# MLP gate and up projections: from feature-major blocks to token-major groups of 512 + 512 columns

## The chip, the cores and the metric

The kernel runs on one core of one Trainium2 chip. The metric is the device time of one execution in microseconds (us). The five engines have queues of their own and run side by side: TensorE (PE) multiplies, VectorE (DVE) and ScalarE (ACT) work element by element, GpSimd (POOL) does a few small things, SyncE (SP) starts most transfers. The kernel is written on a layer that puts in the semaphores and sets the order of the instructions on each engine, with the order of the program as priority.

## The reference, cut to what matters

One encoder layer on 256 tokens, D_MODEL = 2048, D_FF = 5632, all float32:

```python
proj = rms_norm(x, attn_norm) @ w_in                  # 2048 -> 10240, then two attentions ya, yb
merged = sigmoid(ga) * (ya @ w_branch_a) + sigmoid(gb) * (yb @ w_branch_b)
x = x + merged @ w_out
hf = rms_norm(x, ffn_norm)
g = dwconv_centred(hf @ w_ffn_gate, conv_w, conv_b)   # width 3 along the tokens
x = x + (gelu(g) * (hf @ w_ffn_up)) @ w_ffn_down
x = x + sigmoid(rms_norm(x, ple_norm) @ w_ple_gate) * (p @ w_ple_proj)
out = rms_norm(x, final_norm)
```

## The kernel before, in words

**Products from halves.** A float32 operand is split into a high half in the matmul's reduced format and a low half, the difference. A product is then high x high + high x low + low x high. Weights arrive in pieces of 1 MB ([128 x 2048] float32, a ring of three, `raw`), loaded by SP. `produce` (L244) makes each piece's units: ScalarE copies a stretch into a high half (L261), VectorE subtracts it from the weights for the low half (L262). Units stand in a ring of six (`u`), and, for weight differences, a ring of two (`v`). A unit is dropped when its last product is issued, and `pump` (L267) then makes the next ones.

**Two forms of product.** In `block` (L284) the weights are the stationary operand, [128 x 128], and the activations move: 512 columns (high and low half of 256 tokens side by side) for the high weights, 256 for the low ones. The result is feature-major: features in the partitions, tokens along the row. In `thirds` (L321) the activations stand, 128 tokens at a time, and 512 columns of weights move, three matmuls of 512 columns. The result is token-major.

**Seven for eight.** `quad_stage` (L331) works on two output ranges of 512 columns and 256 tokens at once. A piece covers two blocks of 128 rows (k) for both ranges. A plain piece ("s") has 8 products of `thirds`; a piece by seven products ("S") has 7 into seven banks (M1 to M7), but needs differences of the weights (units T13 and T24 from L254 to L256, ring `v`) and sums of the activations (`sums_of`, L780, called `combine` or made on the way). `row_sums` (L750) adds the banks at the stage's last piece and hands each [128 x 512] result to a `finish` function, two or more products after it is done. `at(stage, piece, product)` puts such work at a place in PE's order, `run_due` runs it.

**Stages.** A: the input projection and attention. B0 to B3: the gates in `quad_stage`, B0 all plain, B1 to B3 with the pattern "SsSsSsSs", each followed by the branch products. D0, D1: the output projection, the same pattern; the sums go into `xr`, the residual in token-major rows. Four `turn_back` calls (L803; four transposes of 128 x 128 into bank P22, then copies that split) turn a half of the rows into the feature-major `hf`. E0: half of the MLP's 44 feature chunks; F00, F01: its down projection (11 pieces, "SsSsSsSsSss"); E1, F10, F11 the other half. Then the per-layer embedding (pp, G) and the last norm.

**E before.** `_ffn` (L97) lists gate and up chunks in turn; each is 16 calls of `block` into a bank, 704 a half. `mlp` (L916) gathers the two halves of a bank (ScalarE and VectorE), multiplies by the norm's factor spread over all partitions, does the convolution along the row with per-partition taps, the gelu, the product and the split into `act`, 256 columns at a time. The first four chunks of E0 go side by side, while the second half of `hf` is turned.

Of the kernel before, what the change touches and what calls it, by code (L numbers as in the profile page):

```python
# [32 lines left out]
FHALF = FC // 2  # L33
# [54 lines left out]
JOINT = 4  # L88
# [4 lines left out]
DOWN = "SsSsSsSsSss"  # L93
STANDARD = "s" * 8


def _ffn(half):  # L97

    jobs = []
    for f in range(FHALF + 1):  # L100
        if f < FHALF:
            jobs.append(("g", half * FHALF + f))
        if f:
            jobs.append(("u", half * FHALF + f - 1))
    return jobs


def _pieces():
# [23 lines left out]
    for j in range(4):  # L132
        quads("B%d" % j, ("w_in", GA * P + j * WIDE), ("w_in", GB * P + j * WIDE), ALT if j else STANDARD)
        wide("ba%d" % j, ("w_branch_a", j * WIDE), QH)
        wide("bb%d" % j, ("w_branch_b", j * WIDE), HG)
    for s in range(2):
        quads("D%d" % s, ("w_out", 2 * s * WIDE), ("w_out", (2 * s + 1) * WIDE), ALT)
    for half in range(2):
        names = {"g": "w_ffn_gate", "u": "w_ffn_up"}
        jobs = [(names[kind], f) for kind, f in _ffn(half)]  # L140
        joint = 0 if half else JOINT
        e = [(name, k, f) for k in range(KC) for name, f in jobs[:joint]]
        e += [(name, k, f) for name, f in jobs[joint:] for k in range(KC)]
        blocks("E%d" % half, e)
        for s in range(2):
            quads("F%d%d" % (half, s), ("w_ffn_down", 2 * s * WIDE), ("w_ffn_down", (2 * s + 1) * WIDE),
                  DOWN, half * FHALF)
# [14 lines left out]
def _unit_list():  # L162

    units, of = [], []
    for p, (kind, _) in enumerate(_PIECES):
        if p == 0:
            cuts = [("n", a * P, b * P) for a, b in ((0, 3), (3, 7), (7, 11), (11, PIECE))]
        elif kind == "S":
            cuts = [("n", 0, WIDE), ("n", 2 * WIDE, 4 * WIDE), ("T13", 0, 2 * WIDE), ("T24", 2 * WIDE, 4 * WIDE)]
        else:  # L170
            cuts = [("n", 0, 2 * WIDE), ("n", 2 * WIDE, 4 * WIDE)]
        of.append(list(range(len(units), len(units) + len(cuts))))
        units += [(p, *cut) for cut in cuts]
# [8 lines left out]
RINGS = {"u": 6, "v": 2}  # L182


@with_exitstack
def _encoder(ctx: ExitStack, tc, xt, pt, xrow, cols, gainrow, table, onehot, mask, ident_in, wts, out):
# [57 lines left out]
    def produce():  # L244
# [6 lines left out]
        ring = "u" if kind == "n" else "v"  # L251
# [10 lines left out]
        nc.vector.tensor_tensor(lo, src, hi.bitcast(F32), op=ALU.subtract)  # L262
# [4 lines left out]
    def pump():  # L267
        while not state["early"] and state["unit"] < len(_UNITS):
            p, kind = _UNITS[state["unit"]][:2]
            if state["u" if kind == "n" else "v"] <= 0 or kind != "n" and "tok" not in held:  # L270
                break
# [7 lines left out]
    def drop(u):  # L279
        del made[u]  # L280
        state["u" if _UNITS[u][1] == "n" else "v"] += 1
# [49 lines left out]
    def quad_stage(stage, moving, combos=None, tags=("M2", "M3", "M4", "P22")):  # L331
# [11 lines left out]
        for p in pieces:  # L343
            kind = _PIECES[p][0]
            for name in (list(tags) * 2 if kind == "s" else ["M1", "M7", "M5", "M6", "M2", "M3", "M4"]):
# [10 lines left out]
        for i, p in enumerate(pieces):  # L356
# [3 lines left out]
            if kind == "s":  # L360
# [41 lines left out]
    def gather(acc, scale=1.0, u=None, keep=lambda ins: ins):  # L402

        t = sc.tile([P, T], F32, name="t")
        keep(nc.scalar.activation(t, acc[:, T:], AF.Copy, scale=scale))
        if u is None:
            u = sc.tile([P, T], F32, name="u")
# [17 lines left out]
    def sums(total, columns):  # L425

        s = bank("misc", P, len(columns))
        for c, tokens in enumerate(columns):
            nc.tensor.matmul(s[:, c:c + 1], total[:, tokens], ones[:, :1], start=True, stop=True)
# [10 lines left out]
    def diagonal(r):  # L440

        dg = sc.tile([P, T], F32, name="rdg", bufs=1)
# [4 lines left out]
    def spread(key, dg):  # L447
# [3 lines left out]
        rt[key] = sc.tile([P, T], F32, name="rms", bufs=1)  # L451
# [298 lines left out]
    def row_sums(stage, last, finish, strassen=True, ready=None):  # L750
# [3 lines left out]
        def first():  # L754
            c = outputs()
            if strassen:
                a = held["accs"]
                nc.scalar.activation(c[0][:, cut[0]], a["M1"], AF.Copy)
                nc.vector.tensor_tensor(c[0][:, cut[1]], a["M6"], c[0][:, cut[0]], op=ALU.add)
                nc.vector.tensor_tensor(c[1][:, cut[0]], a["M7"], c[0][:, cut[1]], op=ALU.add)  # L760
                nc.vector.tensor_tensor(c[0][:, cut[1]], a["M5"], c[0][:, cut[1]], op=ALU.add)
                nc.vector.tensor_tensor(c[1][:, cut[1]], a["M5"], c[1][:, cut[0]], op=ALU.add)
# [11 lines left out]
    def quads(stage, moving, combos, finish, strassen=True, ready=None):  # L774
        last = len(_STAGES[stage]) - 1
        row_sums(stage, last, finish, strassen, ready)
# [3 lines left out]
    def sums_of(u, tag):  # L780

        tok = held["tok"]
        f = tok.tile([P, 4, P], F32, name="cmb")
# [12 lines left out]
    def combine(key, m, pair, tag):  # L796

        u = held["tok"].tile([P, 2, T], F32, name="pair", bufs=2)
# [32 lines left out]
    at(("B0", 4, 0), open_tok)  # L831
    for i in range(0, 8, 2):
        at(("B0", 4 + i // 2, 4), combine, "hs", hs, i, i // 2)
    rh = halved(rc[0])

    for j in range(4):

        def gated(t, n, a):
            c = held["c"][t][:, cut[n]]
            if j:  # L840
                nc.vector.tensor_tensor(c, a, c, op=ALU.add)
                a = c
# [7 lines left out]
        quads("B%d" % j, lambda k: hs[:, k, :], lambda i: combos["hs", i], gated, j > 0)  # L850
# [18 lines left out]
    def residual(stage, s, moving, key, square):  # L869
# [14 lines left out]
        quads(stage, moving, lambda i: combos[key, i], finish, True, ready)  # L884
# [18 lines left out]
    for pair, which in enumerate(("M2", "M3", "M4", "P22")):  # L903
        at(("E0", 2 + pair), rows_pair, which, 4 + pair, hf, 1)

    def norm_columns():
        at(("E0", 11), spread, 1, diagonal(rows_root()))

    at(("E0", 8), norm_columns)

    def activation_row(k):
        k %= FHALF
        tile, k = (held["act"][0], k) if k < 16 else (held["act"][1], k - 16) if k < 20 else (held["act"][2], k - 20)
        return tile[:, k, :]

    def mlp(kind, n, acc):  # L916
        tok = held["tok"]
        if kind == "g":
            if n % 2 == 0:
                held["gw"] = tok.tile([P, 4, T], F32, name="gw", tag="c%d" % (n // 2 % 2 + 1))  # L920
            c, w = (held["gw"][:, 2 * (n % 2) + i] for i in range(2))
            u = gather(acc)
            nc.vector.tensor_tensor(u, u, rt[1], op=ALU.mult)
            nc.vector.tensor_scalar(c, u, tap(1, n), tap(3, n), op0=ALU.mult, op1=ALU.add)
            nc.vector.scalar_tensor_tensor(c[:, 1:], u[:, :-1], tap(0, n), c[:, 1:], op0=ALU.mult, op1=ALU.add)
            nc.vector.scalar_tensor_tensor(c[:, :-1], u[:, 1:], tap(2, n), c[:, :-1], op0=ALU.mult, op1=ALU.add)
            nc.scalar.activation(w, c, AF.Square)
            nc.vector.tensor_scalar(w, w, 0.044715, 1.0, op0=ALU.mult, op1=ALU.add)
            nc.vector.tensor_tensor(w, w, c, op=ALU.mult)
            nc.scalar.activation(w, w, AF.Tanh, scale=GELU_C)  # L930
            nc.vector.scalar_tensor_tensor(c, w, 1.0, c, op0=ALU.add, op1=ALU.mult)
            held["gelu", n] = c
        else:
            if n % 2 == 0:
                held["pair"] = tok.tile([P, 2, T], F32, name="pair", bufs=2)
            u = gather(acc, u=held["pair"][:, n % 2])
            nc.vector.scalar_tensor_tensor(u, u, 0.5, rt[1], op0=ALU.mult, op1=ALU.mult)
            nc.vector.tensor_tensor(u, u, held.pop(("gelu", n)), op=ALU.mult)
            halves(activation_row(n), u)
            pair = n % FHALF // 2  # L940
            if n % 2 and DOWN[pair] == "S":
                combos["act", pair] = sums_of(held["pair"], pair // 2)

    for half in range(2):
        held["act"] = [big.tile([P, 16, 2 * T], FR, name="act", tag="R1"),
                       big.tile([P, 4, 2 * T], FR, name="act1", tag="yb"),
                       held["tok"].tile([P, 2, 2 * T], FR, name="act2")]
        jobs = _ffn(half)
        joint = 0 if half else JOINT
        stage = "E%d" % half  # L950
        accs = [bank(which) for which in ("M1", "M5", "M6", "M7")[:joint]]
        for k in range(KC if joint else 0):
            run_due(stage, k)
            for a in accs:
                block(a, hf[:, k, :], k == 0, k == KC - 1)
        for (kind, n), a in zip(jobs, accs):
            mlp(kind, n, a)
        turns["e"] = 0
        for kind, n in jobs[joint:]:
            mlp(kind, n, product(stage, lambda k: hf[:, k, :], KC, "e"))  # L960
        if half:
            pr = held["tok"].tile([P, 2, T], F32, name="pair", bufs=2)
            nc.scalar.dma_start(pr, pt)
            ph_, pl_ = ([sc.tile([P, T], FR, name=name) for _ in range(2)] for name in ("t", "u"))
            for k in range(2):
                nc.scalar.activation(ph_[k], pr[:, k], AF.Copy)
# [137 lines left out]
```

## Time and profile before

| what | us |
|---|---|
| median of 3 runs | 1477.3 (1476.03 to 1477.53) |
| the profiled execution | 1477.12, of which its span 1475.3 |
| TensorE busy | 1456.6 |
| VectorE busy | 1229.5 |
| ScalarE busy | 807.3 |
| E0, by the stage's borders | 246.51 |
| E1 | 244.06 |

A view by windows gives the busy time of each engine in a stretch; the groups by line give the count, the sum and the mean time of one instruction; the timeline gives starts; the chain is followed back from the last instruction. Matmuls are pipelined: the time of one is longer than the step from one to the next.

### The profile page before, as it was taken

Reading aid. Unit: us, or ns where it says so; the run is one execution under the profiler, and the core shown is the slowest. Engines: PE = TensorE matmul, PEld = TensorE weight load, DVE = VectorE, ACT = ScalarE, POOL = GpSimd, SP = SyncE. Lnnn points to the kernel's source line nnn. Section 1 sums busy time; section 2 is a strip of 40 time slices with the busy share of each in tenths; the row PEclk is TensorE's granted clock in tenths of the full one; section 3 lists DMA queues with packets and bytes.
Section 4 is the critical chain, followed back from the end, with each engine's and each line's share of the span. In section 5 each row is a group of like instructions: output and inputs, shape, how many; then the busy total and the mean of one; then the engine's idle time right before and its main releaser. Section 6 shows DMA issues by size and latency. Waiting matters only on the chain.

```text
span 1475.3 us, 20123 instructions
## 1 busy us (share of the span) xinstructions
PE 1456.6 (99%) x7772; PEld 1249.4 (85%) x7772; DVE 1229.5 (83%) x1817; ACT 807.3 (55%) x1142; POOL 4.2 (0%) x9
## 2 busy tenths in 40 slices
PE   9999999999999999999999999999999999999997
PEld 8899999988888887788888888888888888888785
DVE  7587665666989989989888889998888889999994
ACT  7465444444555655665555555554555555565763
POOL 0000000000000000000000000000000000000000
PEclk9999999999999999999999999999999999999998
DMA  9644444445455456475555545465555554446461
GB/s 323 244 158 150 163 172 173 171 171 191 180 199 216 156 212 236 154 253 177 196 196 179 197 171 187 184 254 193 182 198 187 186 199 178 187 184 239 165 237 72
DMA packets 46460, 282.93 MB, mean 192 GB/s; under 512 B 5076, under 2 KB 9812, under 8 KB 14108
## 3 DMA queue, kind: packets, MB, share of 16 engines
q1 hardware_dynamic: 45356, 280.20, 52.2%
q10 hardware_dynamic: 1008, 1.45, 0.3%
q8 instruction: 61, 1.00, 0.3%
q14 instruction: 35, 0.29, 0.1%
HBM read 279.49 MB, written 2.14 MB: 191 GB/s over the span
## 4 chain that ended last, share of the span: by engine, by line
PE 93%; DVE 3%; DMA 2%; issue 1%; ACT 1%; POOLq 0%; ACTq 0%; POOL 0%
PE bank L289 31%; PE bank L290 16%; PE bank L325 13%; PE bank L326 13%; PE bank L324 13%; PE bank L312 2%; PE bank L313 2%; PE bank L314 2%; DMA raw<-in_wts 1%; DVE ul L262 1%; PE bank L808 1%; DVE vl L262 1%; PE bank L628 0%; ACT uh L261 0%; PE bank L575 0%
## 5 line engine op out<-in xcount | busy, mean ns | idle before, releaser
L261 ACT ACTIVATE uh<-raw 128x1024 fp32r<-128x1024 f32 (+2 forms) x518 | 524.1, 1019 | 515.9 <-PE bank L289 278.4
L262 DVE TENSOR_TENSOR ul<-raw,uh 128x1024 fp32r<-128x1024 f32 (+2 forms) x518 | 601.8, 1171 | 199.3 <-ACT uh L261 198.4
L289 PE MATMUL bank<-hf,uh 128*128 128x512 f32 x1408 | 489.2, 393 | 0.0
L290 PE MATMUL bank<-hf,ul 128*128 128x256 f32 x1408 | 392.5, 279 | 0.0
L289 PEld LDWEIGHTS bank<-hf,uh 128*128 128x128 f32 x1408 | 263.7, 187 | 59.4
L290 PEld LDWEIGHTS bank<-hf,ul 128*128 128x128 f32 x1408 | 265.5, 189 | 0.1
L289 PE MATMUL bank<-hs,uh 128*128 128x512 f32 x544 | 194.6, 401 | 1.8 <-DVE hs L422 1.8
L290 PE MATMUL bank<-hs,ul 128*128 128x256 f32 x544 | 152.4, 281 | 0.0
L289 PEld LDWEIGHTS bank<-hs,uh 128*128 128x128 f32 x544 | 102.9, 189 | 25.1 <-DVE hs L422 2.1
L261 ACT ACTIVATE vh<-raw 128x1024 fp32r<-128x1024 f32 x88 | 93.1, 1058 | 48.2 <-DVE raw L256 23.0
L262 DVE TENSOR_TENSOR vl<-raw,vh 128x1024 fp32r<-128x1024 f32 x88 | 107.1, 1218 | 1.6 <-ACT vh L261 0.9
L290 PEld LDWEIGHTS bank<-hs,ul 128*128 128x128 f32 x544 | 103.3, 190 | 0.1
L326 PE MATMUL bank<-uh,act 128*128 128x512 f32 x232 | 90.9, 392 | 0.0
L325 PE MATMUL bank<-ul,act 128*128 128x512 f32 x232 | 90.8, 392 | 0.0
L324 PE MATMUL bank<-uh,act 128*128 128x512 f32 x232 | 90.8, 391 | 0.0
L326 PE MATMUL bank<-uh,hs 128*128 128x512 f32 x184 | 72.2, 392 | 0.0
L325 PE MATMUL bank<-ul,hs 128*128 128x512 f32 x184 | 72.0, 391 | 0.0
L324 PE MATMUL bank<-uh,hs 128*128 128x512 f32 x184 | 72.0, 391 | 0.0
L312 PE MATMUL bank<-uh,hs 128*128 128x256 f32 x224 | 65.0, 290 | 0.0
L314 PE MATMUL bank<-uh,hs 128*128 128x256 f32 x224 | 64.5, 288 | 0.0
L313 PE MATMUL bank<-ul,hs 128*128 128x256 f32 x224 | 64.5, 288 | 0.0
L254 DVE TENSOR_TENSOR raw<-raw 128x1024 f32<-128x1024 f32 x44 | 53.6, 1219 | 0.4
(230 smaller groups left out, 2211.6 us busy)
## 6 DMA issues: line engine op xcount, KB each, us to landing
raw<-in_wts SPq DMA_DIRECT2D x251, 1024.0 KB, 4.8
raw<-in_wts SPq DMA_DIRECT2D x12, 512.0 KB, 6.7
xr<-in_xrow SPq DMA_DIRECT2D x4, 512.0 KB, 9.8
x<-in_xt SPq DMA_DIRECT2D x13, 128.0 KB, 5.7
hb<-hold SPq DMA_DIRECT2D x3, 514.0 KB, 7.8
hb<-hold SPq DMA_DIRECT2D x2, 768.0 KB, 7.6
last<-in_gainrow SPq DMA_DIRECT2D x1, 1024.0 KB, 4.9
out<-xr SPq DMA_DIRECT2D x4, 256.0 KB, 2.6
```

The costliest lines, as they stand in the source:

```text
L254: nc.vector.tensor_tensor(raw[:, :2 * WIDE], raw[:, WIDE:3 * WIDE], raw[:, :2 * WIDE], op=ALU.subtract)
L261: nc.scalar.activation(hi, src, AF.Copy)
L262: nc.vector.tensor_tensor(lo, src, hi.bitcast(F32), op=ALU.subtract)
L289: nc.tensor.matmul(acc, hi[:, w], m, start=first, stop=False, skip_group_check=True)
L290: nc.tensor.matmul(acc[:, T:], lo[:, w], m[:, :T], start=False, stop=last, skip_group_check=True)
L312: nc.tensor.matmul(acc[:, :T], xh, hi, start=(k == 0), stop=False)
L313: nc.tensor.matmul(acc[:, :T], xh, lo, start=False, stop=False)
L314: nc.tensor.matmul(acc[:, :T], xl, hi, start=False, stop=(k == KC - 1))
L324: nc.tensor.matmul(acc, sh, wh, start=first, stop=False)
L325: nc.tensor.matmul(acc, sh, wl, start=False, stop=False)
L326: nc.tensor.matmul(acc, sl, wh, start=False, stop=last)
L808: nc.tensor.transpose(p[:, k, t * P:(t + 1) * P], src(t)[:, k * P:(k + 1) * P], ident)
```

## The change

- The MLP's gate and up become 11 groups (6 in the first half, 5 in the second, `MLP_GROUPS`), each a `quad_stage` of 512 gate and 512 up columns with the pattern `MLP = "SSdsdSds"`. A "d" piece is a plain piece whose second unit gets its low half in another way: ScalarE writes the negated high half, and a transfer on POOL's queue adds the weights from memory to it. `OUTPUT` uses it in D0 and D1.
- `scaled` adds the bank to the row sums and multiplies by the norm's factor, which is per token and so per partition here (the spread factor goes). Four turns (`turned`) bring a group's results back to feature-major, at the first two pieces of the next group, or of F00 and F10 for the last ones. `mixer` and `mixed` do convolution, gelu, product and split, on two chunks at a time, with more of it on ScalarE.
- The down projection has 12 pieces for the first half and 10 for the second, with five S each. Sums of activations for its first two S pieces are made with the group, three more in F00 and F10 (`late`). Sums for `hf` are made in D1, E0 and, for the second half, F01.
- B0 gets two S pieces. In S pieces after the first, the products M2 and M3 come before M7, M5 and M6.
- At the end, the last 512 columns of each token half are worked in two halves, and the multiplication by the gains goes behind the root.

```diff
-DOWN = "SsSsSsSsSss"
-STANDARD = "s" * 8
+FIRST_GATES = "ssssSsSs"
+OUTPUT = "SdSdSdSd"
+MLP = "SSdsdSds"
+DOWN = ("SSsSsSsSssss", "SSsSsSsSss")
+MLP_GROUPS = (range(0, 6), range(6, 11))
...
+    for half, groups in enumerate(MLP_GROUPS):
+        for g in groups:
+            quads("E%d" % g, ("w_ffn_gate", g * WIDE), ("w_ffn_up", g * WIDE), MLP)
...
         nc.scalar.activation(hi, src, AF.Copy)
-        nc.vector.tensor_tensor(lo, src, hi.bitcast(F32), op=ALU.subtract)
+        if kind == "d":
+            nc.scalar.activation(lo, src, AF.Copy, scale=-1.0)
+            nc.gpsimd.dma_start(lo, wts[p][:, a:b], accum_op=ALU.add)
+        else:
+            nc.vector.tensor_tensor(lo, src, hi.bitcast(F32), op=ALU.subtract)
...
+                plain = [("M2", part(b, 0), 1, 1, None), ("M3", sums[3], 1, 0, 1)]
+                mixed = [("M7", sums[2], 2, 1, None), ("M5", sums[0], 2, 0, 2), ("M6", sums[1], 3, 0, None)]
                 for g, (name, stationary, u, c, gone) in enumerate((
-                        ("M1", part(a, 0), 0, 0, 0), ("M7", sums[2], 2, 1, None), ("M5", sums[0], 2, 0, 2),
-                        ("M6", sums[1], 3, 0, None), ("M2", part(b, 0), 1, 1, None), ("M3", sums[3], 1, 0, 1),
+                        ("M1", part(a, 0), 0, 0, 0), *(plain + mixed if i else mixed + plain),
                         ("M4", part(b, 1), 3, 1, 3))):
...
-    at(("B0", 4, 0), open_tok)
-    for i in range(0, 8, 2):
-        at(("B0", 4 + i // 2, 4), combine, "hs", hs, i, i // 2)
+    at(("B0", 3, 0), open_tok)
+    for i, when in ((4, (3, 1)), (6, (3, 6)), (0, (5, 2)), (2, (7, 2))):
+        at(("B0", *when), combine, "hs", hs, i, i // 2)
...
+    at(("D1", 1, 2), combine, "hf", hf, 0, 3)
+    at(("D1", 2, 4), combine, "hf", hf, 1, 4)
...
+    def turned(n, pair, c):
+        p = bank("P22", P, 2, T)
+        for k in range(2):
+            for t in range(2):
+                at_ = n * WIDE + pair * T + k * P
+                nc.tensor.transpose(p[:, k, t * P:(t + 1) * P], c[t][:, at_:at_ + P], ident)
+        u = held["tok"].tile([P, 2, T], F32, name="ut" if n else "gt", bufs=1 if n else 2)
+        nc.scalar.activation(u, p, AF.Copy)
+        return u
+
+    def mixer(f, g):
+        c = held["tok"].tile([P, 2, T], F32, name="cc")
+        for k in range(2):
+            nc.scalar.activation(c[:, k], g[:, k], AF.Identity, scale=tap(1, f + k), bias=tap(3, f + k))
+            nc.vector.scalar_tensor_tensor(c[:, k, 1:], g[:, k, :-1], tap(0, f + k), c[:, k, 1:],
+                                           op0=ALU.mult, op1=ALU.add)
+            nc.vector.scalar_tensor_tensor(c[:, k, :-1], g[:, k, 1:], tap(2, f + k), c[:, k, :-1],
+                                           op0=ALU.mult, op1=ALU.add)
+        nc.scalar.activation(g, c, AF.Square, scale=math.sqrt(0.044715))
+        nc.vector.scalar_tensor_tensor(g, g, 1.0, c, op0=ALU.add, op1=ALU.mult)
+        nc.scalar.activation(g, g, AF.Tanh, scale=GELU_C)
+        nc.vector.scalar_tensor_tensor(c, g, 1.0, c, op0=ALU.add, op1=ALU.mult)
+        return c
+
+    def mixed(half, k, c, u):
+        nc.vector.tensor_tensor(u, u, c, op=ALU.mult)
...
+                nc.scalar.activation(both[:, :, :T], u, AF.Copy)
+                nc.vector.tensor_tensor(both[:, :, T:], u, both[:, :, :T].bitcast(F32), op=ALU.subtract)
+        if k // 2 in held["early"]:
+            combos["act", k // 2] = sums_of(u, held["early"][k // 2])
...
+        for f, pair, when in ((gate, 0, (0, 3)), (gate, 1, (0, 6)), (up, 0, (1, 1)), (up, 1, (1, 5))):
+            at((stage, *when), f, pair)
...
+            def scaled(t, n, a):
+                c = held["c"][t][:, cut[n]]
+                nc.vector.tensor_tensor(c, a, c, op=ALU.add)
+                nc.scalar.activation(c, c, AF.Copy, scale=held["r1"][n][:, t:t + 1])
+            quads("E%d" % g, lambda k: hf[:, k, :], lambda i: combos["hf", i], scaled)
+            group_turns(half, g, "E%d" % (g + 1) if g != groups[-1] else "F%d0" % half, held["c"])
...
+        for pair, tag, when in zip(down_pairs[2:], tags["act"][2:], ((0, 0), (2, 0), (4, 0))):
+            at(("F%d0" % half, *when), late, pair, tag)
...
-        ple(t, 3, accs[t], c[t][:, cut[1]])
+        for h in range(2):
+            cols = slice(3 * WIDE + h * T, 3 * WIDE + (h + 1) * T)
...
         nc.gpsimd.tensor_tensor(r, v, mhalf[:, :1], op=ALU.pow)
+        nc.vector.tensor_tensor(xr[:, t, cut[3]], xr[:, t, cut[3]], gains[:, cut[3]], op=ALU.mult)
```

More of the change, by code (lines that the diff above doesn't have):

```diff
@@ L87 @@
 WARM = 9
-JOINT = 4
 WIDE = 2 * T
@@ L269, in pump @@
             p, kind = _UNITS[state["unit"]][:2]
-            if state["u" if kind == "n" else "v"] <= 0 or kind != "n" and "tok" not in held:
+            ring = "u" if kind in "nd" else "v"
+            if state[ring] <= 0 or ring == "v" and "tok" not in held:
                 break
@@ L916, in mlp @@
[L916 to L942, printed above, removed]
@@ L944, in _encoder, with rows_scale, rows_combine @@
-    for half in range(2):
+    def rows_scale():
+        held["r1"] = rows_root()
+        held["r1"] = (held["r1"], halved(held["r1"]))
+    def rows_combine(stage, pairs, tags, when):
+        for pair, tag, i in zip(pairs, tags, when):
+            at((stage, *i), combine, "hf", hf, pair, tag)
+    mlp_pairs = [i for i, c in enumerate(MLP) if c == "S"]
+    for pair, when in enumerate((("E0", 0, 2), ("E0", 0, 5), ("E0", 1, 0), ("E0", 1, 3))):
+        at(when, rows_pair, "P22", 4 + pair, hf, 1)
@@ new lines, in group_turns, with gate, up @@
+    def group_turns(half, g, stage, c):
+        k = 4 * (g - MLP_GROUPS[half][0])
+        got = {}
+        def gate(pair):
+            got[pair] = turned(0, pair, c)
+            if pair == 0:
+                got["c"] = mixer(4 * g, got[0])
+        def up(pair):
+            u = turned(1, pair, c)
+            mixed(half, k + 2 * pair, got["c"], u)
+            if pair == 0:
+                got["c"] = mixer(4 * g + 2, got[1])
+        for f, pair, when in ((gate, 0, (0, 3)), (gate, 1, (0, 6)), (up, 0, (1, 1)), (up, 1, (1, 5))):
+            at((stage, *when), f, pair)
@@ L949, in _encoder @@
[L949 to L960, printed above, removed]
@@ new lines, in _encoder, with late @@
+        for g in groups:
+            def scaled(t, n, a):
+                c = held["c"][t][:, cut[n]]
+                nc.vector.tensor_tensor(c, a, c, op=ALU.add)
+                nc.scalar.activation(c, c, AF.Copy, scale=held["r1"][n][:, t:t + 1])
+            quads("E%d" % g, lambda k: hf[:, k, :], lambda i: combos["hf", i], scaled)
+            group_turns(half, g, "E%d" % (g + 1) if g != groups[-1] else "F%d0" % half, held["c"])
+        def late(pair, tag):
+            u = held["tok"].tile([P, 2, T], F32, name="ut")
+            rows = [activation_row(2 * pair + i).bitcast(F32) for i in range(2)]
+            for i in range(2):
+                nc.vector.tensor_tensor(u[:, i], rows[i][:, :T], rows[i][:, T:], op=ALU.add)
+            combos["act", pair] = sums_of(u, tag)
@@ L973, in _encoder @@
                 at(when, rows_pair, "P22", pair, pl, 2)
-            at(("F11", 2, 4), combine, "pl", pl, 0, 0)
-            at(("F11", 4, 4), combine, "pl", pl, 2, 1)
+            at(("F11", 2, 4), combine, "pl", pl, 0, tags["next"][0])
+            at(("F11", 4, 4), combine, "pl", pl, 2, tags["next"][1])
+        else:
+            for pair, tag, when in zip(mlp_pairs, tags["next"], ((2, 4), (4, 4), (6, 4))):
+                at(("F01", *when), combine, "hf", hf, pair, tag)
         residual("F%d1" % half, 1, activation_row, "act", half)
```

129 lines of the change are left out of this document (61 added, 68 removed).

## The prediction, made before the result

> **What bounds the kernel now.** I read the page first: busy time by engine, then the chain that ended last.
>
> ```profile
> span 1475.3 us, 20123 instructions
> ...
> PE 1456.6 (99%) x7772; PEld 1249.4 (85%) x7772; DVE 1229.5 (83%) x1817; ACT 807.3 (55%) x1142; POOL 4.2 (0%) x9
> ...
> PE 93%; DVE 3%; DMA 2%; issue 1%; ACT 1%; POOLq 0%; ACTq 0%; POOL 0%
> ```
>
> TensorE is busy 99% of the span and is 93% of the chain. So the time is, to first order, what PE has to stream; the other engines matter where they make PE wait. To see where that is, I cut the span at the stages' borders (B1, D0, D1, E0, F00, E1, F11 in this order) and asked for the busy time in each.
>
> ```profile
> core 0: us, PE busy (x) PEld busy (x) DVE busy (x) ACT busy (x) POOL busy (x), PEclk, DMA share, GB/s
> 378.88:421.30 42.42, 42.42 (x190) 34.38 (x188) 39.88 (x49) 24.61 (x28) 0.00 (x0) 1.00 0.62 232
> ...
> 555.03:599.34 44.31, 42.64 (x190) 34.28 (x188) 40.88 (x50) 25.13 (x28) 0.00 (x0) 1.00 0.58 219
> 599.34:643.88 44.54, 43.57 (x197) 35.14 (x196) 43.65 (x52) 27.53 (x36) 0.00 (x0) 1.00 0.56 205
> 643.88:890.39 246.51, 246.51 (x1427) 215.56 (x1426) 214.30 (x392) 134.73 (x215) 0.70 (x1) 1.00 0.53 188
> 890.39:947.64 57.25, 57.25 (x252) 46.69 (x250) 52.76 (x62) 32.30 (x37) 0.00 (x0) 1.00 0.54 198
> ...
> 1004.88:1248.94 244.06, 244.06 (x1409) 215.26 (x1408) 209.23 (x375) 128.57 (x202) 0.00 (x0) 1.00 0.52 187
> ...
> 1306.16:1365.76 59.60, 59.52 (x267) 48.12 (x266) 58.20 (x76) 35.55 (x46) 0.00 (x0) 1.00 0.58 219
> ```
>
> The clock is granted in full in all of them (PEclk 1.00). E0 and E1, which the change rewrites, take 246.51 + 244.06 = 490.57 us, all of it PE work. Next, what a product costs when nothing is waited for: these are the first and last of 18 products in a row (timeline of PE).
>
> ```profile
> 639.80 0.39 PE L324 MATMUL bank<-uh,merged 128*128 128x512 f32 x1
> ...
> 643.66 0.39 PE L326 MATMUL bank<-uh,merged 128*128 128x512 f32 x1
> ```
>
> 17 steps in 3.86 us: 0.2271 us for 512 columns, though each lasts 0.39; the steps are the price. A turn back (four transposes) stands in the chain, and by the piece in the groups by line:
>
> ```profile
> 1311.66 0.44 PE bank L808 x4
> ```
> ```profile
> L808 PE MATMUL bank<-ident,xr 128*128 128x128 f32 x64 | 9.7, 272 | 0.0
> ```
>
> Four cost 0.44, not 4 x 0.272, since they overlap. With these two prices each stage is checked. F00 has 249 products, 56.55 us, and took 57.25: the 0.70 over belongs to its five pieces by seven products ("S"), 0.14 each. B1: 180 x 0.2271 + 4 x 0.14 + 2 turns = 42.3, took 42.42. F11: 249 products, five S, four turns, 59.0, took 59.60. D0: 42.3, took 44.31; D1: 43.2, took 44.54. So the stalls are 0.1, 0.6, 2.0 and 1.3 us, and they come with VectorE's load: 39.88 of 42.42 in B1, 43.65 of 44.54 in D1.
>
> **The MLP's products.** Before, each 128x128 weight block is a stationary operand with a 512- and a 256-column product:
>
> ```profile
> L289 PE MATMUL bank<-hf,uh 128*128 128x512 f32 x1408 | 489.2, 393 | 0.0
> L290 PE MATMUL bank<-hf,ul 128*128 128x256 f32 x1408 | 392.5, 279 | 0.0
> ```
>
> 1408 pairs. After: 11 groups of three S pieces (7 products of three matmuls) and five plain ones (8 of three), 63 + 120 = 183 matmuls a group, 2013 in all, 457.2 us at 0.2271. Added: 33 S pieces x 0.14 = 4.6; four turns a group, 44 x 0.44 = 19.4 (the last group of each half has its turns in F). E0 keeps its own four turns of the rows, 1.8. Sum 483.0 against 490.57: **-7.6 us**, the whole of what PE gains here: columns saved by seven-for-eight are mostly paid out again as transposes.
>
> **What VectorE gets for it.** Its prices, back to back, from its timeline in F00 (starts 1.13, 0.60 and 1.14 apart), and groups by line, in E1 and in the whole span:
>
> ```profile
> 905.11 1.22 DVE L262 TENSOR_TENSOR ul<-raw,uh 128x1024 fp32r<-128x1024 f32 x1
> 906.24 0.69 DVE L256 TENSOR_TENSOR raw<-raw 128x512 f32<-128x512 f32 x1
> 906.84 1.22 DVE L262 TENSOR_TENSOR vl<-raw,vh 128x1024 fp32r<-128x1024 f32 x1
> 907.98 1.22 DVE L262 TENSOR_TENSOR ul<-raw,uh 128x1024 fp32r<-128x1024 f32 x1
> ```
> ```profile
> L925 DVE SCALAR_TENSOR_TENSOR gw<-u,cl,gw 128x255 f32<-128x255 f32 x22 | 10.6, 482 | 0.5
> ```
> ```profile
> L261 ACT ACTIVATE vh<-raw 128x1024 fp32r<-128x1024 f32 x88 | 93.1, 1058 | 48.2 <-DVE raw L256 23.0 <-DVE raw L254 15.3 <-PE bank L326 9.8
> ...
> L785 DVE TENSOR_TENSOR cmb<-pair 128x128 f32<-128x128 f32 x22 | 6.2, 284 | 0.1
> ```
>
> So 1.135 for 1024 columns, 0.60 for 512, and, taking 0.08 off the duration as in these, about 0.40 for the 255-wide taps and 0.20 for 128. An S piece: one low half of 512, three of 1024, differences of 1024, 512, 512: 6.34. A group: three S 19.0; three "d" pieces (one low half on VectorE, the other by transfer) 3.4; two plain 4.5; row sums and the four `scaled` adds 4.8; two mixers (four taps, two of 512) 5.6; two `mixed` (two of 512) 2.4. Together **39.7 us** under PE's 183 x 0.2271 + 0.4 + 1.8 = **43.7**. By full durations (1.22, 0.69, 0.48) it is 44.4. The truth lies between: VectorE at 91 to 101%, where E1 shows 209.23 of 244.06. ScalarE makes 25 copies of units (3x4 + 3x3 + 2x2, three of them 512 wide) in 25 us, and the turns' copies, scaling, squares and tanh are an estimated 11 us by their widths: 36 of 43.7, no bound. What hides VectorE is the ring of six weight units. In E0 the producer waits for PE, not PE for it:
>
> ```profile
> ACT uh L261 <- PE bank L289: 103.1, 82, 1.7
> ```
>
> In D1 a row sum came late, and PE waited:
>
> ```profile
> PE bank L324 <- DVE xr L879: 1.0, 1, 1.0
> ```
>
> A group border has the same form: bank P22 must be emptied by the last `scaled` add before the first turn, three products later (2.0 us). I take 0.3 us of stall a group, between B1's 0.1 and F11's 0.6: **+3.3** (1.1 to 14 with D1's 1.3).
>
> [...]
>
> **F stages.** The counts of products stay: 2 x 91 + 2 x 75 = 332, as 4 x 83 before. But the S pieces move forward ("SSsSsSs..."), and F00 and F10 inherit the last group's mixers (8.0) and three `late` sums (two of 256, four of 128, one of 512: 2.1 each). Up to the sixth piece VectorE has 36.6 us of work (rest of the second S 4.6, S 6.34 twice, plain 2.27 twice, late 6.2, mixers and `mixed` 8.0, a row sum 0.6), 2.3 of it possible ahead, and PE 30.9 (126 matmuls, three S, four turns). Over by 3.4 at most in each of two stages; the mixers' rows are needed only by the last pieces and can be put off, so I take 1.0 each: **+2** (0 to 7).
>
> **D stages.** Four low halves of each leave VectorE (4.5 us), D1 takes in two combines of 2.0 (0.60, four of 0.20, 0.60). In D0 PE stalled because a load could only start when late halves had freed its buffer:
>
> ```profile
> 552.70 7.45 DMA raw<-in_wts
> ...
> 564.91 0.61 DVE merged L812
> 565.56 0.65 PE bank L808 x4
> ```
>
> I take half of the 3.3 us of stall: **-1.6** (-3.3 to +2).
>
> **The transfers.** 41 low halves come by a negating copy on ScalarE and an accumulating transfer from POOL's queue. The transfer waits for the copy; behind it on POOL stand the next transfers and one root for the norm, due three pieces later; PE waits for its data. No accumulating transfer is in the trace. The nearest rows:
>
> ```profile
> raw<-in_wts SPq DMA_DIRECT2D x251, 1024.0 KB, 4.8
> ...
> xr<-in_xrow SPq DMA_DIRECT2D x4, 512.0 KB, 9.8
> ```
>
> The group's first d unit gets its slot when the group before ends and is used 45 matmuls and the turns later: 12.3 us, less three copies of 1.06, leaves 9. So 4.8 is hidden, 9.8 is late by 1. I take the first, whose traffic is the same stage's: nothing. Raw loads share the engines (0.53 busy, B1 ran at 0.62 unhindered).
>
> [...]
>
> **B0 and the tail.** Two plain pieces become S: 6 matmuls less, **-1.1** after 2 x 0.14 (their combines need memory that the attention holds until the piece before: -1.4 to +1.5). The tail, after PE's last product:
>
> ```profile
> 1465.22 0.69 ACT L1018 ACTIVATE c<-bank,rh 128x512 f32<-128x512 f32 x1 [0.43 <-ACT xr L1046]
> ...
> 1468.15 0.69 DVE L1022 TENSOR_TENSOR xr<-xr,last 128x512 f32<-128x512 f32 x1 [0.79 <-ACT c L1021]
> 1468.76 0.21 DVE L1040 TENSOR_SCALAR v<-ssq,known 128x1 f32<-128x1 f32 x1
> ```
>
> The gain multiply (0.6) goes behind the root, and halves overlap on two engines, 0.3: **-0.9** (-1.2 to 0).
>
> **Sum.** The profiled execution took 1477.12 us, the median is 1477.3. -7.6 + 3.3 + 2 - 1.6 - 1.1 - 0.9 = -5.9: **1471.2 us**. What a measurement can tell from no change is 0.2%, 3 us.
>
> **Rivals.**
> *The stalls eat it.* At D1's class of stall, 0.8 a group, E's gain is gone: 5.5 more, 1476.7. For it: VectorE over 91% with ScalarE at 82% instead of 53%; against: B1 at 94% with 0.1.
> *VectorE becomes the bound (slower).* From 43.7 us a group on, E follows it: at full durations 11 x 44.4 + 1.8 = 490.2, F late by 7, D by 2: -0.4 + 7 + 2 - 1.1 - 0.9 = +6.6, 1483.7. For it: the front-loaded F stages; against: back-to-back starts in F00.
> *The transferred halves land late.* At 9.8 and with the turns' copies ahead of the negation on ScalarE, 2 us a group is 22: 1493. For it: a kind not seen here; against: the ring, and 4.8.
>
> **How the numbers follow.** Forecast 0.53 (down to 1464.7, all stalls at their least), eaten 0.20, VectorE 0.17, transfers 0.10. Forecast is faster, eaten is the same, the other two slower: 0.53, 0.20, 0.27. The range from 1464.7 to 1488 leaves out most of the transfers' case and some 0.08 beside.
>
> **What would show it.** Right: groups 44 us apart, PE without idle in them, VectorE at 40 to 43 of 44, turns at 0.44, d transfers landing in 5 to 8 us. Wrong: PE idle ended by a d unit's `ul` or its transfer; PE idle ended by `vl` or `c` in F00, F10; groups of over 44.6 us; products above 0.2271 us where transfers run.

## The result and the profile after

The changed kernel takes 1604.29 us (1600.99 to 1606.04) against 1477.41 (1476.03 to 1477.91) of the kernel before beside it: 1.085 times as long, with a 95% interval of 1.083 to 1.087. The profiled execution took 1606.04, of which its span is 1604.3. The prediction of 1471.2, and its range, are far off.

The page of the kernel after: span, busy time by engine, PE and its granted clock in 40 slices, the engines' shares of the chain, the costliest wait among the groups by line, and two transfers with their size and median time to landing.

```profile
span 1604.3 us, 18996 instructions
...
PE 1489.8 (93%) x7137; PEld 1233.7 (77%) x7137; DVE 1298.2 (81%) x1747; ACT 936.9 (58%) x1253; POOL 40.8 (3%) x50
...
PE   9999999999999989778888999999968889989997
...
PEclk9999999999999999989999999999988999999999
...
PE 66%; DMA 14%; DVE 10%; issue 7%; ACT 2%; POOL 0%; POOLq 0%; ACTq 0%; DVEq 0%; SPq 0%
...
L317 PE MATMUL bank<-ul,hf 128*128 128x512 f32 x506 | 208.3, 412 | 66.9 <-DMA ul<-in_wts 66.9
...
raw<-in_wts SPq DMA_DIRECT2D x251, 1024.0 KB, 5.6
ul<-in_wts POOLq DMA_DIRECT2D x41, 512.0 KB, 9.0
```

Two things are new. PE stands idle for 1604.3 - 1489.8 = 114.5 us, where it was 18.7, and the transfer of low halves is the one thing named. And PE is busy 33.2 us longer, with 635 fewer matmuls: the second row, PEclk, has two dents. Both are in the stages with transfers, as the view by windows shows (D0, D1, E0, E3, F00, E7, F11):

```profile
core 0: us, PE busy (x) PEld busy (x) DVE busy (x) ACT busy (x) POOL busy (x), PEclk, DMA share, GB/s
...
553.39:604.68 51.29, 45.83 (x189) 36.61 (x188) 37.61 (x47) 28.11 (x32) 3.49 (x4) 0.93 0.81 251
604.68:663.59 58.91, 49.28 (x198) 38.50 (x196) 44.11 (x62) 31.99 (x43) 2.61 (x3) 0.88 0.53 159
663.59:724.07 60.48, 48.69 (x201) 38.23 (x199) 42.91 (x61) 30.14 (x40) 3.36 (x4) 0.92 0.52 167
831.73:881.48 49.75, 45.36 (x201) 36.69 (x200) 39.06 (x50) 33.53 (x45) 2.62 (x3) 0.97 0.61 201
...
976.47:1044.92 68.45, 66.10 (x290) 52.02 (x289) 68.11 (x94) 43.32 (x57) 0.00 (x0) 1.00 0.48 185
1153.29:1216.67 63.38, 49.35 (x200) 39.43 (x199) 42.41 (x60) 34.04 (x46) 2.62 (x3) 0.87 0.44 141
...
1434.86:1495.09 60.23, 56.42 (x242) 44.45 (x241) 59.15 (x76) 35.31 (x46) 0.00 (x0) 0.97 0.48 183
```

A group takes 46 to 63 us instead of the 44 forecast, and the clock in it is as low as 0.87. By stages the 129.0 us between the spans divide so: the eleven groups 580.9 where E0 and E1 were 490.6 (+90.4), D0 and D1 110.2 where they were 88.9 (+21.4), the four F stages 250.6 where they were 231.3 (+19.3), all else -2.1.

One wait in full. In E7 PE's timeline (start, length, and in brackets the idle time and what ended it) reads:

```profile
1165.23 0.60 PE L921 MATMUL bank<-ident,c 128*128 128x128 f32 x4
1173.59 0.80 PE L317 MATMUL bank<-ul,hf 128*128 128x512 f32 x1 [7.76 <-DMA ul<-in_wts]
1174.18 0.63 PE L318 MATMUL bank<-uh,hf 128*128 128x512 f32 x1
1174.61 0.63 PE L316 MATMUL bank<-uh,hf 128*128 128x512 f32 x1
1175.03 0.63 PE L317 MATMUL bank<-ul,hf 128*128 128x512 f32 x1
```

After 7.76 us without work the products come 0.43 apart instead of 0.2271, until 1179.6: this wait cost more than its length. The records of the granted clock hold 17 such stretches at half between 565 and 1446 us, 92 us together, each 3.41, 6.83 or 10.24 long, and each begins in a wait of PE (of 1.27 to 7.76 us) or at most 0.81 us behind one. PE is busy for 72 of these 92 us, so an estimate of what half clock cost is half of that, 36 us.

The waits by line say how much of PE's idle time transfers ended (total, times, longest), in PE's weight loads and its products, which overlap:

```profile
PEld bank L317 <- DMA ul<-in_wts: 87.4, 22, 8.0
...
PE bank L317 <- DMA ul<-in_wts: 79.0, 20, 7.8
```

So about half of the 41 transfers are late. Why the third piece's was late in E3 (the group starts at 831.73; its unit is wanted at 844.3) is in ScalarE's timeline, then POOL's and PE's:

```profile
832.22 0.71 ACT L987 ACTIVATE c<-c,rr 128x512 f32<-128x512 f32 x1
832.83 1.04 ACT L248 ACTIVATE uh<-raw 128x1024 fp32r<-128x1024 f32 x1
833.78 0.71 ACT L987 ACTIVATE c<-c,rh 128x512 f32<-128x512 f32 x1
...
835.73 0.60 ACT L923 ACTIVATE gt<-bank 128x512 f32<-128x512 f32 x1
836.23 1.05 ACT L248 ACTIVATE vh<-raw 128x1024 fp32r<-128x1024 f32 x1
837.17 1.08 ACT L930 ACTIVATE cc<-gt,cl 128x256 f32<-128x256 f32 x2
838.16 0.58 ACT L923 ACTIVATE gt<-bank 128x512 f32<-128x512 f32 x1
838.64 1.05 ACT L250 ACTIVATE ul<-raw 128x1024 fp32r<-128x1024 f32 x1
```
```profile
840.09 0.86 POOL L251 DMA_DIRECT2D ul<-in_wts  x1 [29.44 <-DVE cc L931]
```
```profile
848.92 0.79 PE L317 MATMUL bank<-ul,hf 128*128 128x512 f32 x1 [4.39 <-DMA ul<-in_wts]
```

The high half is copied from 832.83 on; the negated copy (L250) starts 5.81 later, behind scalings, a turn's copy and the convolution's first tap. Issue is 8.4 us after the border, landing 8.8 after the issue, and PE waits for 4.39. The copy of L250 ends at 839.7, 0.4 ahead of the issue.

### The profile page after: what moved, and what is told of

Read it like the earlier page. It is cut to its first block, busy times and chain, and to the rows that moved or that the text cites. A ratio compares the mean times of both kernels' runs of the same rounds, so it can differ in the third digit from the quotient of the medians.

```text
span 1604.3 us, 18996 instructions
## 1 busy us (share of the span) xinstructions
PE 1489.8 (93%) x7137; PEld 1233.7 (77%) x7137; DVE 1298.2 (81%) x1747; ACT 936.9 (58%) x1253; POOL 40.8 (3%) x50
## 4 chain that ended last, share of the span: by engine, by line
PE 66%; DMA 14%; DVE 10%; issue 7%; ACT 2%; POOL 0%; POOLq 0%; ACTq 0%; DVEq 0%; SPq 0%
PE bank L317 16%; PE bank L318 15%; PE bank L316 15%; DMA ul<-in_wts 11%; PE bank L281 8%; PE bank L282 4%; DVE ul L253 3%; DMA raw<-in_wts 2%; PE bank L304 2%; PE bank L305 2%; PE bank L306 2%; DVE vl L253 2%; ACT uh L248 1%; DVE raw L241 1%; DVE raw L242 1%
## 5 line engine op out<-in xcount | busy, mean ns | idle before, releaser
L253 DVE TENSOR_TENSOR ul<-raw,uh 128x1024 fp32r<-128x1024 f32 (+2 forms) x477 | 531.8, 1127 | 218.6 <-ACT uh L248 217.8
L317 PE MATMUL bank<-ul,hf 128*128 128x512 f32 x506 | 208.3, 412 | 66.9 <-DMA ul<-in_wts 66.9
L248 ACT ACTIVATE vh<-raw 128x1024 fp32r<-128x1024 f32 x158 | 166.4, 1054 | 86.6 <-DVE raw L241 48.1
L318 PE MATMUL bank<-uh,hf 128*128 128x512 f32 x506 | 205.9, 408 | 0.0
L316 PE MATMUL bank<-uh,hf 128*128 128x512 f32 x506 | 202.5, 403 | 0.0
L253 DVE TENSOR_TENSOR vl<-raw,vh 128x1024 fp32r<-128x1024 f32 x158 | 192.4, 1219 | 8.6 <-ACT vh L248 8.1
L317 PEld LDWEIGHTS bank<-ul,hf 128*128 128x128 f32 x506 | 100.2, 198 | 94.7 <-DMA ul<-in_wts 73.5
L318 PEld LDWEIGHTS bank<-uh,hf 128*128 128x128 f32 x506 | 100.3, 198 | 20.9
L316 PEld LDWEIGHTS bank<-uh,hf 128*128 128x128 f32 x506 | 99.2, 196 | 21.9 <-DVE xr L870 0.4
L317 PE MATMUL bank<-vl,S 128*128 128x512 f32 x237 | 96.0, 405 | 1.4 <-DVE vl L253 1.3
L241 DVE TENSOR_TENSOR raw<-raw 128x1024 f32<-128x1024 f32 x79 | 96.2, 1218 | 0.7
L318 PE MATMUL bank<-vh,S 128*128 128x512 f32 x237 | 94.2, 398 | 0.0
L316 PE MATMUL bank<-vh,S 128*128 128x512 f32 x237 | 91.8, 399 | 1.7 <-ACT vh L248 1.2
L318 PE MATMUL bank<-uh,act 128*128 128x512 f32 x232 | 90.4, 392 | 0.0
## 6 DMA issues: line engine op xcount, KB each, us to landing
xr<-in_xrow SPq DMA_DIRECT2D x4, 512.0 KB, 12.3
```

What stands on the lines that cost most here:

```text
L241: nc.vector.tensor_tensor(raw[:, :2 * WIDE], raw[:, WIDE:3 * WIDE], raw[:, :2 * WIDE], op=ALU.subtract)
L248: nc.scalar.activation(hi, src, AF.Copy)
L316: nc.tensor.matmul(acc, sh, wh, start=first, stop=False)
L317: nc.tensor.matmul(acc, sh, wl, start=False, stop=False)
L318: nc.tensor.matmul(acc, sl, wh, start=False, stop=last)
```

## The experiments

Theory T: the accumulating transfers land late, and each late one costs its wait and a stretch at half clock. Rivals: VectorE's theory, that the groups' work on VectorE holds PE up whether transfers run or not; and B, that the transfers take bandwidth from the loads of weights. Each experiment is an edit of the kernel after, unless it says otherwise; ratios are to the kernel before, on the same chip.

**no_transfer.** All low halves by VectorE.

```diff
-OUTPUT = "SdSdSdSd"
-MLP = "SSdsdSds"
+OUTPUT = ALT
+MLP = "SSsssSss"
```


> The changed kernel with the d pieces made plain again (MLP SSsssSss, D stages SsSsSsSs): every low half comes from VectorE. Theory T (the accumulating transfers arrive late, and each long wait also halves the granted clock for some us): the waits for ul by transfer are gone, the clock is back at 0.99, the time is 1475 to 1500. Rival V (VectorE and ScalarE are overloaded by the groups, the transfers only show it): the same waits come back as waits for ul by VectorE, the time stays at 1590 or more. Rival B (the transfers' traffic delays the weight loads): 1475 to 1500 too, and ScalarE's waits for raw fall from 110 us to below 60.

Measured: 1509.18 us (1508.09 to 1509.59), ratio 1.0219 (1.0199 to 1.0238). 95 of the 127 us go with the transfers; 33 stay, more than T left. D1, E0, E2 and F10:

```profile
core 0: us, PE busy (x) PEld busy (x) DVE busy (x) ACT busy (x) POOL busy (x), PEclk, DMA share, GB/s
596.16:641.18 45.02, 43.57 (x197) 34.92 (x196) 44.29 (x62) 26.83 (x38) 0.00 (x0) 1.00 0.46 173
641.18:693.34 52.16, 47.55 (x201) 37.14 (x200) 47.83 (x65) 28.79 (x38) 0.71 (x1) 0.93 0.44 170
737.76:783.55 45.79, 45.03 (x201) 35.12 (x199) 44.05 (x57) 30.25 (x41) 0.00 (x0) 1.00 0.50 184
...
1275.01:1336.54 61.53, 57.02 (x242) 42.55 (x241) 61.11 (x89) 39.23 (x53) 0.00 (x0) 1.00 0.47 175
```

VectorE is busy for 44.05 of 45.79 in E2 and 61.11 of 61.53 in F10: here it is the bound. PE's largest waits, summed over the span, are now for units of the S pieces: its weight loads wait 20.7 us, 32 times, for ScalarE's copy `vh`, and that copy waits 38.9 us for VectorE's differences of the weights. ScalarE's wait for loads of `raw` rose, from 109.8 us in the kernel after to 164.8, which speaks against B.

**mlp_transfers.** Transfers in the MLP alone (`OUTPUT = ALT`).

> The changed kernel with d pieces in the MLP alone, D0 and D1 as before (SsSsSsSs). T: D0 and D1 fall from 110.2 us together to 87 to 92, the rest keeps its time: 1578 to 1588. V: D0 and D1 keep at least 100 us: 1594 or more.

Measured: 1598.08 (1594.56 to 1602.67), 1.0829 (1.0794 to 1.0864). D0 and D1 fell by 20.8 to 89.4, as expected, but the total by 6 only: E0 rose from 60.5 to 67.6, and the groups' waits for transfers are 72.5 us in PE's products, against 66.9 in the kernel after. The expected total was missed. At E0's start PE now waits four times, 0.4 to 1.2 us each, three times for VectorE and once for ScalarE's copy `vh`; no_transfer has the same four waits (0.8 to 1.4 us, with the clock of its E0 at 0.93), the kernel after one (1.20). VectorE is busy for 44.66 of 45.42 us in D1 here, for 44.11 of 58.91 there. That fits a VectorE that had caught up during D's idle time in the kernel after. A transfer saved in D is not a wait saved.

**negated_first.** The negated copy and the transfer stand ahead of the high copy in the program.

```diff
-        nc.scalar.activation(hi, src, AF.Copy)
         if kind == "d":
             nc.scalar.activation(lo, src, AF.Copy, scale=-1.0)
             nc.gpsimd.dma_start(lo, wts[p][:, a:b], accum_op=ALU.add)
-        else:
+        nc.scalar.activation(hi, src, AF.Copy)
+        if kind != "d":
```


> The changed kernel with the negated copy and the transfer ahead of the high half's copy in program order. In the trace 1 to 7 us pass between the high half's start and the issue of the transfer. T: each transfer is issued 1 to 6 us earlier, the waits of 66.9 us shrink by 20 to 60 us with their slow clock: 1530 to 1580. V and B: 1598 to 1608, nothing changes.

Measured: 1598.3 (1596.79 to 1602.77), 1.0828 (1.0802 to 1.0854). That lies in the rivals' range, but the issue hardly moved: in E3 it still came 8.4 us after the border, since the order on ScalarE put the copy behind the same work. This doesn't answer its question.

**plain_transfer.** The transfer copies instead of adding, without a negated copy. The low halves of those units hold the whole weights: the subtraction is left out.

```diff
-            nc.scalar.activation(lo, src, AF.Copy, scale=-1.0)
-            nc.gpsimd.dma_start(lo, wts[p][:, a:b], accum_op=ALU.add)
+            nc.gpsimd.dma_start(lo, wts[p][:, a:b])
```


> The changed kernel where the transfer of a d unit copies the weights instead of adding them: no negated copy ahead of it, the destination isn't read. The low half then holds whole weights, so nothing is subtracted. T, if the time before the issue is what makes it late: a transfer can start when its slot is free, the waits fall below 10 us, 1480 to 1500. B (the traffic): the same bytes from memory, so at least 1560. If the transfer's own length (8 to 10 us to landing) is what counts: landing stays at 8 to 10 us, and the waits fall only as far as the issue is earlier.

Measured: 1492.6 (1490.65 to 1496.28), 1.011 (1.0086 to 1.0134). The transfer's row on the page, and the window of E2:

```profile
ul<-in_wts POOLq DMA_DIRECT2D x41, 512.0 KB, 4.0
```
```profile
739.98:783.58 43.60, 43.60 (x201) 35.89 (x199) 41.55 (x54) 30.50 (x42) 1.60 (x3) 1.00 0.61 228
```

The same bytes from the same queue land in 4.0 us and PE never waits for them. B falls. E1 to E5, E9 and E10 take 43.6 to 43.9, the floor that the prediction worked out (43.7): its price of products and turns holds (E7 and E8 take 45.1). What is late is the accumulating kind: 5 us longer, and behind a copy. The edit takes away both at once, so it doesn't tell their shares. E0 keeps 52.20 and F11 60.43.

**pool_negation.** The negated copy on GpSimd.

```diff
-            nc.scalar.activation(lo, src, AF.Copy, scale=-1.0)
+            nc.gpsimd.tensor_scalar(lo, src, -1.0, None, op0=ALU.mult)
```


> The changed kernel with the negated copy on GpSimd, which has nothing else to do, instead of ScalarE, where it stood behind the group border's work (issue of a group's first transfer 8 us after the border). T: it is issued as soon as its slot and the weights are there, 3 to 5 us after the border; landing stays near 9 us; the waits for transferred halves fall below 25 us in all, the clock rises to 0.985 or more: 1510 to 1550. If only the transfer's length counts: the waits stay above 60 us, 1590 or more.

Measured: 1545.35 (1542.04 to 1551.12), 1.0464 (1.0432 to 1.0497), as expected. The copy takes 3.0 us at the median there (2.8 to 7.3) instead of 1.05, and yet PE's products wait 25.6 us for transfers instead of 79.0, on a queue with little else in it; landing takes 7.6 instead of 9.0. E2 to E5 take 45.2 to 46.6. 59 of the 95 us come back with the accumulation kept, so ScalarE's queue is a large part of the lateness.

**late_transfers.** On two_of_eight (below), transfers in each group's last two pieces, away from the border's work.

```diff
-MLP = "SSssssss"
+MLP = "SSssssdd"
```


> two_of_eight with its last two pieces of each group by transfer (SSssssdd), 22 transfers, all away from the group's border. The theory that the border's work on ScalarE delays the negated copy: issue is early enough there, groups stay at 44.3 to 45 us and the time at 1487 to 1494. The rival, that an accumulating transfer is late wherever it stands: PE waits for ul in most groups, 1 to 3 us each and then at half clock, over 1505.

Measured: 1514.59 (1508.59 to 1517.65), 1.0247 (1.0224 to 1.0269), 24 more than two_of_eight: the rival's case. PE waits in every group, for one of its two transfers. In E2, by ScalarE, POOL and PE:

```profile
774.44 1.99 ACT L248 ACTIVATE uh<-raw 128x1024 fp32r<-128x1024 f32 x2
776.33 0.62 ACT L937 ACTIVATE gt<-gt 128x512 f32<-128x512 f32 x1
776.85 1.05 ACT L250 ACTIVATE ul<-raw 128x1024 fp32r<-128x1024 f32 x1
```
```profile
778.25 0.89 POOL L251 DMA_DIRECT2D ul<-in_wts  x1 [42.44 <-ACT ul L250]
```
```profile
788.67 0.54 PE L317 MATMUL bank<-ul,hf 128*128 128x512 f32 x1 [2.30 <-DMA ul<-in_wts]
789.01 0.63 PE L318 MATMUL bank<-uh,hf 128*128 128x512 f32 x1
789.43 0.63 PE L316 MATMUL bank<-uh,hf 128*128 128x512 f32 x1
```

The unit's own copy starts at 775.4 (the second of two), and PE wants the unit at 786.2, when the product before it (785.98) is streamed. That is the lead of the ring of six: 10.8 us. The chain of copy (0.9), a gelu step that came between (0.5), negated copy (1.05), issue (0.35) and landing (10.4) needs 13.2. Here the border isn't to blame. An accumulating low half is late even in a quieter place (the idle time before it is 0.4 to 2.3 us in E1 to E10 and 5.6 in E0), and the work at the border adds its 5.

**filled_waits.** 14 unused products, 3.2 us, stand in the program before the third piece of each group, to keep PE busy.

```diff
+                if kind == "d" and stage[0] == "E" and i == 2:
+                    idle = bank("P22")
+                    for _ in range(14):
+                        nc.tensor.matmul(idle, a[:, :P], a, start=True, stop=True)
```


> The changed kernel with 14 products that nobody uses (3.2 us) on PE ahead of the third piece of each MLP group, where PE waits 2 to 8 us for the first transfer. T with the clock: PE is idle for shorter, the clock in E0 to E5 and E7 to E10 rises from 0.87 to 0.97 to at least 0.97, and the time falls by 10 to 30 us although nothing comes earlier: 1574 to 1594. If the clock is no cause of its own: the products fill what was idle, or add where no wait was: 1600 to 1640.

Measured: 1631.07 (1629.0 to 1632.89), 1.1045 (1.1019 to 1.107): slower by 27, where 10 to 30 less was expected; that is the rival's range. But the products don't run where the edit wants them. In E3 PE's timeline reads:

```profile
854.31 0.79 PE L317 MATMUL bank<-ul,hf 128*128 128x512 f32 x1 [7.47 <-DMA ul<-in_wts]
...
863.03 3.34 PE L356 MATMUL bank<-hf 128*128 128x512 f32 x14
```

They come 8.7 us behind the wait, and in every group that waits there they come 5.4 to 9.4 us behind it; in E6 there is no wait at that place. (They need bank P22, which the turns of the first two pieces use; that this put them off is likely, not shown.) So no wait was filled: the waits stayed (80.1 us in PE's products), and so did the clock, 0.970 for 0.968. Whether the clock's half could be saved by filling is not settled by it; that part is read from the trace alone.

**alternating_down.** The 33 us that no_transfer leaves: on no_transfer, the down projection's S pieces every second piece again.

```diff
-DOWN = ("SSsSsSsSssss", "SSsSsSsSss")
+DOWN = ("SsSsSsSsSsss", "SsSsSsSsSs")
```


> no_transfer with the down projection's S pieces alternating (SsSsSsSsSsss, SsSsSsSsSs) as before, instead of SSsSsSs first. Theory: the front-loaded S pieces hold up F00, F10 and F11 by 7 us each; they go to 66 to 68, 55 to 57 and 54 to 57 us (from 71.9, 61.5, 60.7): 1490 to 1500. Rival: the last group's mixers and the late sums do it whatever the order: F stages within 2 us, 1505 to 1511.

Measured: 1507.49 (1504.36 to 1510.07), 1.0203 (1.0179 to 1.0227). F00 70.1, F10 60.3, F11 60.7: within 2 us of no_transfer. The front-loaded pattern isn't the cause.

**two_of_eight.** On alternating_down, two S pieces a group instead of three (three matmuls more a group, some 4 us of VectorE's work less).

```diff
-MLP = "SSsssSss"
+MLP = "SSssssss"
```


> alternating_down with two S pieces a group instead of three (SSssssss), no transfers. PE has 0.54 us more a group, VectorE 4.1 less. Theory V for what is left (VectorE at 43.1 of 43.7 us holds up the groups): groups of 44.4 us instead of 45.2, E0 3 us less: 5 to 15 us under alternating_down. Rival (PE alone): 6 us over it.

Measured: 1490.31 (1489.52 to 1491.46), 1.0088 (1.0069 to 1.0108), 17 less. The windows of E0, E2, F10 and F11:

```profile
core 0: us, PE busy (x) PEld busy (x) DVE busy (x) ACT busy (x) POOL busy (x), PEclk, DMA share, GB/s
641.18:694.54 53.36, 49.43 (x204) 38.39 (x202) 47.62 (x64) 28.25 (x37) 0.70 (x1) 0.90 0.45 168
738.85:783.16 44.31, 44.31 (x204) 36.35 (x202) 41.30 (x56) 29.82 (x41) 0.00 (x0) 1.00 0.52 190
1264.02:1317.53 53.51, 53.51 (x242) 43.49 (x241) 53.12 (x75) 35.59 (x49) 0.00 (x0) 1.00 0.49 183
1317.53:1380.01 62.48, 58.73 (x243) 46.40 (x241) 59.53 (x77) 34.64 (x45) 0.00 (x0) 0.92 0.53 201
```

With VectorE at 41.30 of 44.31 a group has no idle time, and F10, which inherited a backlog, has none either. Two places are left: E0 and F11, each some 9 us over its work and at 0.90 and 0.92 of the clock. In the stage before each, VectorE has no rest: 44.30 of 45.02 in D1 and 53.12 of 53.51 in F10.

**relieved_borders.** On two_of_eight, one S less in the stage ahead of each: D1, and F10 with F11.

```diff
-        quads("D%d" % s, ..., OUTPUT)
+        quads("D%d" % s, ..., "SsSsSsss" if s else OUTPUT)
-DOWN = ("SsSsSsSsSsss", "SsSsSsSsSs")
+DOWN = ("SsSsSsSsSsss", "SsSsSsSsss")
```


> two_of_eight with one S piece less in D1 (SsSsSsss) and in F10 and F11 (SsSsSsSsss). The theory that VectorE's backlog at two borders is what is left: E0 falls from 53.4 us to 45 to 48, F11 from 62.5 to 54 to 57, while D1 and F10 pay 1.2 each for the six products more; 1476 to 1483 in all, from 1490.3. The rival, that the first units of E0 and F11 wait for the turns at those borders whatever VectorE has to do: E0 and F11 stay (F11 1.2 longer), about 1494.

Measured: 1476.3 (1473.33 to 1479.16) against 1476.77, ratio 0.9992 (0.9981 to 1.0003): 14 less than two_of_eight. (The expectation's six products for an S less are three, so each of the three stages pays 0.5 and not 1.2.) E0, E2 and F11:

```profile
640.78:686.78 46.00, 44.88 (x203) 36.27 (x202) 42.65 (x58) 26.86 (x36) 0.70 (x1) 1.00 0.48 183
731.08:775.46 44.38, 44.38 (x203) 36.37 (x202) 41.29 (x56) 29.83 (x41) 0.00 (x0) 1.00 0.52 190
...
1310.36:1365.13 54.77, 54.46 (x246) 44.06 (x244) 53.83 (x71) 31.91 (x43) 0.00 (x0) 1.00 0.60 232
```

E0 falls by 7.4 and F11 by 7.7, at full clock, as VectorE's theory had it. E0's own pieces are unchanged; F11 gave up an S piece too, so its fall isn't the work of F10 alone. VectorE's share of the stage ahead doesn't show the difference: it is busy for 45.09 of 45.82 us in D1 and 53.59 of 54.01 in F10, as full as in two_of_eight. The token-major MLP without its losses is level with the kernel before, not below it.

**small_parts.** The kernel before with three of the change's small edits alone: two S pieces in B0, the other order of products, the tail in halves.

> The kernel before with only the two S pieces in B0, the other order of products in S pieces and the tail in halves. By the stage times of the kernel after: B0 1.3 less, B1 to B3 0.2 each, G0 0.7, the tail 0.5, so 1473.5 to 1475 against 1476.7. The rival, that those came from other edits of the change (its memory layout, its pools): within 0.5 us of the kernel before.

Measured: 1475.46 (1473.26 to 1478.48), 0.9989 (0.9978 to 1.0). In its profile B0 takes 46.48 (47.76 before) and G0 41.14 (42.08), but D1 46.25 (44.55). That is 1.3 us faster, at the edge of what can be told. relieved_borders holds these edits too, so its 1476.3 is not the MLP's alone.

## Why the prediction was wrong

**The transfers, "I take the first ... nothing": failed.** This is the step that decides. no_transfer puts it at 95 us. The rows taken for it, 4.8 and 9.8, were of plain loads. The accumulating kind took 9.0 at the median (5.4 to 12.4), the plain kind of the same size 4.0 from the same queue; that 9.8 comes near is chance. The sum of 12.3 less three copies also failed: at the border the negation waits for 5 us of other work, and away from it the ring's lead is 10.8, with 13.2 to be done. The working let the copies stand directly behind each other, as if ScalarE at 82% had no queue.

**The rival "The transferred halves land late": the right mechanism at a fifth of its size.** It had 2 us a group and 1493. Waits are up to 7.8, and the rival had no price for what follows a wait, the stretches at half clock, some 36 us by the estimate above.

**Group stalls, +3.3 (1.1 to 14): too small.** Without transfers, E1 to E5 and E7 to E10 of no_transfer sum to 405.5, where nine floors of 43.7 make 393.3: 1.4 a group, not 0.3. E0 has 8 more. The rival "VectorE becomes the bound" was half of the truth: with three transfers a group it is busy for 42.3 to 42.4 us in E4 and E5, between the forecast's 39.7 and 44.4. Without them VectorE has 44 of 45.8, and PE follows it. ("The stalls eat it" calls 0.8 a group D1's class of stall. D1's own was 1.3, which would have made 1482.)

**F stages, +2 (0 to 7): failed.** The four stages took 250.6. The forecast for them is 231.3, plus 3.5 for the last groups' eight turns, plus 2: 236.8. Working "over by 3.4 at most" took VectorE as rested at each stage's start. It enters F00 and F10 with a backlog, and F11 inherits F10's: alternating_down shows that the pattern isn't to blame, two_of_eight and relieved_borders that the load is.

**D stages, -1.6: failed in the kernel after** (+21.4, transfers again); without transfers D0 and D1 are 88.5 where they were 88.9.

**Held:** the products and turns (floor of 43.7, measured 43.6 to 43.9 in seven groups of plain_transfer); B0, -1.3 for -1.1; the tail, from the last product's start to the end of the span 10.3 us where it was 11.2, -0.9 as forecast.

What stays open: how much of the half-clock stretches a busier PE would have avoided (filled_waits filled no wait), and how the lateness divides between the accumulation and the copy ahead of it.

## What to carry to other kernels

A transfer that replaces an engine's work must be priced with the whole chain up to it (copy, its place in that engine's queue, issue, landing) against the lead that the ring of buffers gives (13.2 us against 10.8 in late_transfers); a landing time of another kind of transfer is no price for it (4.0 us plain, 9.0 accumulating). A stall of TensorE can cost more than its length, where a stretch at half clock follows (in E7 of the kernel after, products 0.43 us apart instead of 0.2271 for 6 us behind the wait of 7.76). And an engine without rest in one stage handed its backlog to the next (one S piece less in D1, and E0 fell by 7.4 us). Its share of busy time doesn't show how large that is (VectorE had 98% of D1 in two_of_eight and in relieved_borders), so the first waits behind a border are where to look, and the stage ahead is where to take load off.

## What the runs showed of the hardware

- An accumulating transfer of 512 KB from memory, started by GpSimd, landed in 9.0 us at the median in the kernel after (7.6 in pool_negation, 9.8 in late_transfers), a plain one from the same queue in 4.0 in plain_transfer; starting one occupied GpSimd for 0.87 us in the kernel after.
- Half clock came with short waits too, and not with every long one. In E0 of two_of_eight half clock began 0.6 us after the second of two waits of 0.85 and 1.20 us and lasted for 10.24, with two more waits (0.69 and 1.20) inside it; in late_transfers single waits of 1.8 us in E1 and 2.3 in E2 were followed by 3.4 each (clock 0.96 in both), one of 0.4 in E4 by none (1.00). In the kernel after, waits of 0.43 and 1.27 us in E4 came with 3.41 at half clock, one of 3.38 in E2 with none.
- GpSimd's multiplication by a constant on [128 x 1024] took 3.0 us at the median (2.8 to 7.3), ScalarE's copy of the same 1.05.
